# A two-layer encoder trunk: another order of work where the up projections pass into the down projections

## The chip, the cores and the metric

The kernel runs on one core of one Trainium2 chip. A core has TensorE (PE, matrix products), VectorE (DVE), ScalarE (ACT), GpSimd (POOL) and SyncE (SP, whose queue starts most transfers), each with an instruction stream of its own that runs in order; they meet at semaphores. The metric is device time in microseconds (us) of one execution. Before the change three runs gave a median of 2614.29 us (2614.18 to 2615.53).

## The reference, cut to what matters

Each of two layers is a token mixer (attention in the first, a gated delta rule in the second) followed by a dense MLP. The change is at one place inside the MLP, which runs once per layer:

```python
def squared_relu_mlp(h, w_up, w_down):
    return jnp.square(jax.nn.relu(h @ w_up)) @ w_down

x = x + squared_relu_mlp(rmsnorm(x, mlp_norm[i]), mlp_w_up[i], mlp_w_down[i])
```

x is 1024 tokens by 1024, w_up 1024 by 4096, w_down 4096 by 1024, all float32.

## The kernel before

**Products.** Every float32 matrix is split into a high part (rounded by ACT, method `high`, L1017) and a low part (the rest, a subtraction on DVE, method `low`, L1014, or on POOL, L1012). A product of two such matrices is three matmuls: high by high, high by low, low by high. Big products are done in 2 by 2 blocks with seven block products in place of eight, so sums and differences of blocks are needed on both sides: of the weights (`s1` to `s4`, made on POOL by `padd`, L1023, and `psub`, L1020, then split), and of the activations (`t1` to `t4`).

**Up.** `up` works through 16 groups (n = 0 to 15) of 256 of the 4096 hidden features. A group ends with four blocks of squared activations `g`. Three of them go to DRAM as they are (`gr`, issued by ACT); `combine` makes the four sums of them: POOL subtracts (L1020), ACT takes the high part (L1017), DVE the low part (L1093), and SP stores both to DRAM (`gt`, L1094), 512 KB each. The sums of group n are made beside the products of group n+1. Those of the last group, n = 15, have no next group: `block` hands them to `down` as the generator `late`.

**Down.** `down` has 32 units: 8 blocks b of hidden features by 4 pairs u of output panels. A unit has seven block products of 6 matmuls, called slots here: Y 11, Z s1, Y s2, X 12, Y s3, Z s4, Y 22. After each slot, `step` (L1377) lets every side job go one step: `late`, then `work` (loads and splits of the activations of block b+1, method `rows`), then `more` (the weights of the unit after this one, `down_weights`); only then does DVE add the slot's result from PSUM to x (L1419). So whatever a step gives to DVE stands ahead of that addition in DVE's stream. Y collects several products in one PSUM tile, and a slot on Y can start only when DVE has read the tile for the slot before on Y. In slot Z s1 of each unit the low part of the next unit's first weights (`wlo`) is given to DVE ahead of the additions of Z s1 and Y s2. Unit weights arrive as a 512 KB tile `wraw` by SP (L1227); there are two such buffers.

**The passage.** The rows of block b = 0 and the weights of unit 0 are made during the last up group, by the generator `tail` in `block`, one of whose steps is taken at seven places of `up` (method `end`) and one right after it. Its last step asks for the first four x tiles (L2505, 512 KB each); `down` then asks for the weights of unit 1. Each x tile takes the buffer of a sum of group 14, so its load must wait until that sum is stored. The order of SP's queue is set when the program is built; the order on the other engines is that of the code. SP's stream is in order too: an entry that waits for another engine holds all loads and stores behind it.

Of the kernel before, what the change touches and what calls it, by code (L numbers as in the profile page):

```python
# [8 lines left out]
F32 = mybir.dt.float32  # L9
F32R = mybir.dt.float32r  # L10
I32 = mybir.dt.int32
AF = mybir.ActivationFunctionType
ALU = mybir.AluOpType
# [4 lines left out]
P = 128  # L18
D = 1024
S = 1024  # L20
KT = D // P
HB = 512
# [186 lines left out]
class Trunk:  # L209
# [871 lines left out]
    def combine(self, n, g, mp, gt):  # L1081

        nc = self.nc
        t = {z: mp.tile([P, S], F32, name=self.nm("c"), tag=f"x{4 * (n % 2) + k}") for k, z in enumerate(SUMS)}

        def sub(z, x, y):
            self.psub(t[z][:, HB:], x, y)

        def high(z):
            self.high(t[z][:, :HB].bitcast(F32R), t[z][:, HB:])  # L1090

        def low(z):
            nc.vector.tensor_tensor(t[z][:, HB:].bitcast(F32R), t[z][:, HB:], t[z][:, :HB], ALU.subtract)  # L1093
            nc.sync.dma_start(gt[n, SUMS.index(z)], t[z])  # L1094

        sub("t1", g[0, 1], g[0, 0])
        sub("t3", g[1, 1], g[0, 1])
        yield
        sub("t2", g[1, 1], t["t1"][:, HB:])
        sub("t4", g[1, 0], t["t2"][:, HB:])  # L1100
        high("t1")
        yield
        high("t3")
        low("t1")
        yield
        high("t2")
        low("t3")
        yield
        high("t4")
        low("t2")  # L1110
        yield
        low("t4")
        yield
# [107 lines left out]
            A, rest = nxt, more  # L1221
        return sums

    def down_weights(self, i, b, u, ap, A, keep=False):

        raw = self.wp.tile([P, 4, 2, P], F32, name=self.nm("wraw"), tag="wraw")
        self.wq.dma_start(raw, self.a["w_down"][i, b, u])  # L1227
        yield
        hi, lo = (self.wp.tile([P, 4, 2, P], F32R, name=self.nm("w" + z), tag="w" + z) for z in ("hi", "lo"))

        def kept(tag, n=2):
            return [x[:, : n * 2 * P].rearrange("p (n k m) -> p n k m", n=n, k=2) for x in self.part(self.hp, tag)]

        h42, l42 = kept(f"{2 * u}0") if keep else (hi[:, 2:4], lo[:, 2:4])
        A["11"], A["12"] = ((hi[:, n], lo[:, n]) for n in range(2))
        A["s4"], A["22"] = ((h42[:, n], l42[:, n]) for n in range(2))

        self.high(hi[:, 0:2], raw[:, 0:2])
        if keep and u:
            s31, s2 = (x.bitcast(F32) for x in kept(f"{u}1"))  # L1240
            s2 = s2[:, 0]
        else:
            s31 = ap.tile([P, 2, 2, P], F32, name=self.nm("s"), tag="a0")
            s2 = ap.tile([P, 2, P], F32, name=self.nm("s"), tag="a1")
        self.padd(s31[:, 1], raw[:, 2], raw[:, 3])
        self.psub(s2, s31[:, 1], raw[:, 0])
        yield

        self.low(lo[:, 0:2], raw[:, 0:2], hi[:, 0:2])
        yield  # L1250

        yield

        if keep and u:
            A["s2"] = tuple(x[:, 0] for x in kept(f"{(0, 4, 5, 0)[u]}1"))
        else:
            A["s2"] = tuple(ap.tile([P, 2, P], F32R, name=self.nm("a"), tag=f"a{4 + n}") for n in range(2))
        self.high(A["s2"][0], s2)
        self.psub(s31[:, 0], raw[:, 0], raw[:, 2])
        self.psub(raw[:, 2], raw[:, 1], s2)  # L1260
        yield

        self.low(A["s2"][1], s2, A["s2"][0])
        yield

        if keep and u:
            h31, l31 = kept(f"{2 * u + 1}0")
        else:
            h31, l31 = (ap.tile([P, 2, 2, P], F32R, name=self.nm("a"), tag=f"a{2 + n}") for n in range(2))
        A["s3"], A["s1"] = ((h31[:, n], l31[:, n]) for n in range(2))  # L1270
        self.high(h31, s31)
        yield

        self.low(l31, s31, h31, b == 7)
        self.high(h42, raw[:, 2:4])
        yield

        self.low(l42, raw[:, 2:4], h42, b == 7)
        yield
# [82 lines left out]
    def down(self, i, hx, mq, xs, late, gr, gt, ops, first, after, ahead, norm):  # L1362

        nc = self.nc
        units = [(b, u) for b in range(8) for u in range(4)]

        def add(x, y):
            nc.vector.tensor_tensor(x, y, x, ALU.add)

        A, rest = first  # L1370
        nxt = {}
        more = self.down_weights(i, *units[1], hx, nxt)
        next(more)
        work, part = None, None
        ready, doing, at = [], [], [0]

        def step():  # L1377

            at[0] += 1
            early = not part and (G["m_order"] >> (at[0] - 1) % 14) & 1  # L1380
            if early:
                next(more, None)
            next(late, None)
            next(work, None)
            if part:
                for d in doing:
                    next(d)
                doing.clear()
                if ready:
                    x, k, h = ready.pop(0)  # L1390
                    d = part(x, k, h)
                    next(d)
                    doing.append(d)
            if not early:
                next(more, None)
            if n >= 30:
                next(ahead, None)

        for n, (b, u) in enumerate(units):
            if u == 0:  # L1400
                work = iter(())
                if b < 7:
                    work = self.rows(hx, gr, gt, b + 1, ops[(b + 1) % 2])
                else:
                    part = after()
                B = ops[b % 2]
            if norm and b == 7:
                after_next, more = more, iter(())
                next(rest)
                self.down_end(i, hx, mq, xs, B, {0: A, 1: nxt}, {1: after_next}, part, norm)  # L1410
                break
            x11, x12, x21, x22 = (xs[2 * u + m][:, h * HB : (h + 1) * HB] for m in range(2) for h in range(2))
            X = self.bank()
            Y, Z = (mq.tile([P, HB], F32, name=self.nm(z), tag=z) for z in "yz")

            def slot(ps, l, r, first, last, x, k=None, h=None):
                self.block_product(ps, A[l], B[r], first, last)
                step()
                nc.vector.tensor_tensor(x, ps, x, ALU.add)  # L1419
                if part and k is not None:  # L1420
                    ready.append((x, 2 * u + k, h))

            next(rest, None)
            slot(Y, "11", "11", True, False, x11)
            if n < len(units) - 1:
                slot(Z, "s1", "t1", True, False, x22)
                slot(Y, "s2", "t2", False, False, x12)
                slot(X, "12", "21", True, True, x11, 0, 0)
                slot(Y, "s3", "t3", False, False, x22, 1, 1)
                slot(Z, "s4", "22", False, True, x12, 0, 1)  # L1430
                slot(Y, "22", "t4", False, True, x21, 1, 0)
            else:
                slot(X, "12", "21", True, True, x11, 0, 0)
                slot(Y, "s2", "t2", False, False, x12)
                slot(Z, "s1", "t1", True, False, x22)
                slot(Y, "s3", "t3", False, False, x22, 1, 1)
                slot(Z, "s4", "22", False, True, x12, 0, 1)
                slot(Y, "22", "t4", False, True, x21, 1, 0)
            A, rest = nxt, more
            nxt, more = {}, iter(())  # L1440
            if n + 2 < len(units):
                more = self.down_weights(i, *units[n + 2], hx, nxt, bool(norm) and n + 2 >= 28)
                next(more)
        while ready or doing:
            step()
        for _ in ahead:
            pass
# [69 lines left out]
    def block(self, i, rhs, x, w, which, after, done=None, ahead=iter(()), norm=None):  # L1517
# [5 lines left out]
        with tc.tile_pool(name=f"xa{i}", bufs=1) as xa, tc.tile_pool(name=f"xb{i}", bufs=1) as xb, \  # L1523
# [12 lines left out]
            def tail():  # L1536
                rows = self.first_rows(xp, ex, gr, gt, B[0])
                got["A"] = {}
                got["rest"] = weights = self.down_weights(i, 0, 0, hx, got["A"])
                for steps in (1, 1, 2, 1, 2, 1):  # L1540
                    next(rows, None)
                    for _ in range(steps):
                        next(weights)
                    yield
                next(rows, None)
                got["xs"] = self.load_x(xp, xd, range(4))
                yield

            def late():
# [5 lines left out]
            with tc.manual_schedule(engines=ENG):  # L1555
                self.out_proj(w, rhs, xs, tile_done, finish, rest)
                sums = self.up(i, ops, hx, xp, yz, gr, gt, finish, A, rest, end)
                next(end)
                self.down(i, hx, yz, got["xs"], chain(sums, late()), gr, gt, B, (got["A"], got["rest"]),
                          after, ahead, norm)  # L1560
                if done:
                    done(got["xs"])
# [996 lines left out]
```

## Time and profile before

| | |
|---|---|
| runs, median of 3 | 2614.29 us |
| profiled execution, its own time | 2614.47 us |
| its span | 2612.4 us |
| PE busy | 2476.4 us, 95% |
| DVE / ACT / POOL busy | 1922.9 (74%) / 1211.8 (46%) / 1320.8 us (51%) |
| chain that ended last, by engine | PE 76%, DVE 12%, DMA 4%, issue 3%, POOL 2%, ACT 2% |
| passage of the first layer | near 880 to 930 us |
| passage of the second layer | near 2260 to 2310 us |

The last up group of the first layer ends near 889 us and the first unit of `down` begins there; the same work comes again in the second layer near 2268 us. In a row of a timeline the bracket at the end gives how long the engine sat idle before that work and which work ended the wait. The column PEclk is the clock granted to TensorE, 1.00 for 2.4 GHz and 0.50 for 1.2 GHz.

### The profile page before, as it was taken

Reading aid. Unit: us, or ns where it says so; the run is one execution under the profiler, and the core shown is the slowest. Engines: PE = TensorE matmul, PEld = TensorE weight load, DVE = VectorE, ACT = ScalarE, POOL = GpSimd, SP = SyncE. Lnnn points to the kernel's source line nnn. Section 1 sums busy time; section 2 is a strip of 40 time slices with the busy share of each in tenths; the row PEclk is TensorE's granted clock in tenths of the full one; section 3 lists DMA queues with packets and bytes.
Section 4 is the critical chain, followed back from the end, with each engine's and each line's share of the span. In section 5 each row is a group of like instructions: output and inputs, shape, how many; then the busy total and the mean of one; then the engine's idle time right before and its main releaser. Section 6 shows DMA issues by size and latency. Waiting matters only on the chain.

```text
span 2612.4 us, 36716 instructions
## 1 busy us (share of the span) xinstructions
PE 2476.4 (95%) x12638; PEld 2067.2 (79%) x12638; DVE 1922.9 (74%) x3287; ACT 1211.8 (46%) x2269; POOL 1320.8 (51%) x1100
## 2 busy tenths in 40 slices
PE   8999999989999899998888999999889999899997
PEld 6888888877888678886666788888777888688885
DVE  6665656677878778878578976676677787778887
ACT  5666667534555433234673343343335455533333
POOL 2444456236676656565464333332225666565656
PEclk9999999999999999999998999999999999999998
DMA  4222224315555876643443121222324555876652
GB/s 159 69 67 77 60 84 155 116 73 181 213 208 207 309 261 203 230 145 108 117 139 111 55 73 59 68 81 105 105 89 157 206 214 207 301 265 221 215 164 81
DMA packets 189050, 389.28 MB, mean 149 GB/s; under 512 B 54512, under 2 KB 61104, under 8 KB 188864
## 3 DMA queue, kind: packets, MB, share of 16 engines
q1 hardware_dynamic: 172592, 353.36, 39.9%
q10 hardware_dynamic: 16272, 33.58, 3.3%
q8 instruction: 99, 1.62, 0.3%
q14 instruction: 87, 0.71, 0.1%
HBM read 251.96 MB, written 126.52 MB: 145 GB/s over the span
## 4 chain that ended last, share of the span: by engine, by line
PE 76%; DVE 12%; DMA 4%; issue 3%; POOL 2%; ACT 2%; SPq 1%; DVEq 0%; ACTq 0%; POOLq 0%
PE y L1008 23%; PE acc L164 17%; PE z L1008 11%; PE acc L1008 6%; PE tp L164 3%; PE s L164 3%; PE po L164 2%; PE pt L164 2%; PE sp L164 2%; PE acc L279 2%; PE acc L280 2%; PE acc L278 2%; DVE ft L164 2%; DVE wlo L1014 1%; DMA xs<-gt 1%
## 5 line engine op out<-in xcount | busy, mean ns | idle before, releaser
L164 PE MATMUL acc<-xs,whi 128*128 128x512 f32 x1808 | 629.1, 411 | 9.7 <-DVE xp L164 7.2
L164 PEld LDWEIGHTS acc<-xs,whi 128*128 128x128 f32 x1808 | 331.6, 190 | 59.0 <-DVE xp L164 7.9
L164 PE MATMUL acc<-xs,wlo 128*128 128x512 f32 x896 | 367.0, 410 | 2.8 <-POOL wlo L164 2.8
L1008 PE MATMUL y<-xs,whi 128*128 128x512 f32 x1008 | 316.9, 396 | 9.2 <-DVE ssum L1127 9.2
L164 POOL TENSOR_TENSOR wlo<-wraw,whi 128x512 fp32r<-128x512 f32 x126 | 167.7, 1331 | 246.3 <-ACT whi L164 197.9
L1023 POOL TENSOR_TENSOR s<-wraw 128x256 f32<-128x256 f32 (+1 forms) x93 | 91.4, 983 | 357.9 <-DVE a L1014 180.4
L1014 DVE TENSOR_TENSOR wlo<-wraw,whi 128x512 fp32r<-128x512 f32 (+1 forms) x184 | 212.5, 1155 | 44.6 <-ACT whi L1017 44.6
L1008 PEld LDWEIGHTS y<-xs,whi 128*128 128x128 f32 x1008 | 192.9, 192 | 51.0 <-DVE ssum L1127 10.4
L1008 PE MATMUL y<-xs,a 128*128 128x512 f32 x732 | 192.0, 398 | 22.9 <-DVE x L1419 22.9
L1008 PE MATMUL y<-xs,wlo 128*128 128x512 f32 x504 | 200.0, 397 | 12.9 <-DVE wlo L1014 12.9
L1017 ACT ACTIVATE whi<-wraw 128x512 fp32r<-128x512 f32 (+2 forms) x191 | 146.4, 767 | 129.9 <-PE y L1008 83.7
L1419 DVE TENSOR_TENSOR x<-y,x 128x512 f32<-128x512 f32 x240 | 165.4, 689 | 41.1 <-PE y L1008 27.8
L1017 ACT ACTIVATE a<-s 128x256 fp32r<-128x256 f32 x122 | 64.0, 525 | 282.6 <-PE y L1008 167.0
L164 PEld LDWEIGHTS acc<-xs,wlo 128*128 128x128 f32 x896 | 170.7, 190 | 28.3 <-POOL wlo L164 4.4
L1008 PEld LDWEIGHTS y<-xs,a 128*128 128x128 f32 x732 | 139.0, 191 | 56.7 <-DVE x L1419 25.7
L1093 DVE TENSOR_TENSOR c<-c 128x512 fp32r<-128x512 f32 x128 | 151.9, 1206 | 36.2 <-POOL c L1020 35.7
L1008 PE MATMUL acc<-xs,whi 128*128 128x512 f32 x528 | 164.2, 392 | 0.0
L1008 PE MATMUL y<-xs,ahi 128*128 128x512 f32 x512 | 158.6, 391 | 2.0 <-ACT nt L1148 2.0
L164 POOL TENSOR_SCALAR pr<-pr,rs 128x640 f32<-128x640 f32 (+4 forms) x128 | 88.1, 691 | 129.2 <-DVE rs L164 98.1
L1008 PE MATMUL z<-xs,whi 128*128 128x512 f32 x480 | 150.3, 395 | 0.0
L164 POOL TENSOR_TENSOR cy<-cy,cz 128x512 f32<-128x512 f32 x48 | 68.9, 1436 | 144.4 <-DVE cz L164 131.0
L1020 POOL TENSOR_TENSOR c<-g,ssum 128x512 f32<-128x512 f32 x32 | 41.4, 1295 | 184.4 <-ACT g L1130 179.4
(320 smaller groups left out, 6341.0 us busy)
## 6 DMA issues: line engine op xcount, KB each, us to landing
gt<-c SPq DMA_DIRECT2D x128, 512.0 KB, 2.8
xs<-gt SPq DMA_DIRECT2D x256, 256.0 KB, 4.4
wraw<-in_w_up_dram SPq DMA_DIRECT2D x64, 512.0 KB, 3.4
wraw<-in_w_down_dram SPq DMA_DIRECT2D x64, 512.0 KB, 4.3
r<-gr SPq DMA_DIRECT2D x96, 256.0 KB, 3.1
gr<-ssum ACTq DMA_DIRECT2D x64, 256.0 KB, 2.3
wraw<-in_w_in_dram SPq DMA_DIRECT2D x32, 512.0 KB, 3.4
wraw<-in_w_qkv_dram SPq DMA_DIRECT2D x30, 512.0 KB, 3.3
```

Source lines behind the costliest of these rows:

```text
L164: return call(*args, **more)
L278: nc.tensor.matmul(ps, hi[:, k], xh, start=(k == 0), stop=False)
L279: nc.tensor.matmul(ps, hi[:, k], xl, start=False, stop=False)
L280: nc.tensor.matmul(ps, lo[:, k], xh, start=False, stop=(k == KT - 1))
L1008: nc.tensor.matmul(ps, w[:, k], x, start=bool(first and f), stop=bool(last and e), skip_group_check=True)
L1014: self.nc.vector.tensor_tensor(lo, src, hi.bitcast(F32), ALU.subtract)
L1017: self.nc.scalar.activation(hi, src, AF.Copy)
L1020: self.nc.gpsimd.tensor_tensor(out, x, y, ALU.subtract)
L1023: self.nc.gpsimd.tensor_tensor(out, x, y, ALU.add)
L1093: nc.vector.tensor_tensor(t[z][:, HB:].bitcast(F32R), t[z][:, HB:], t[z][:, :HB], ALU.subtract)
L1419: nc.vector.tensor_tensor(x, ps, x, ALU.add)
```

## The change

It has five parts, all at the passage, in both layers:

- `down_weights` gets a branch for unit 0 (`start=True`): the same sums, high and low parts, but the four POOL operations in a row, then s2 and the s1/s3 pair split first, the plain blocks last. `tail` takes one step of it per step of its own.
- `tail` asks for x tiles 0 and 1 after its fifth step, then for the weights of unit 1, then for x tiles 2 and 3. `down` gets unit 1's weights handed in instead of asking for them.
- `late` (the sums of group 15, then x tiles 4 to 7) starts at `down`'s third step instead of its first.
- In `combine`, for group 15 alone, the low parts of `t1` and `t3` move from DVE to POOL.
- Nothing is left out or added in the arithmetic; PE's order stays as it was.

```diff
@@ combine
         def low(z):
-            nc.vector.tensor_tensor(t[z][:, HB:].bitcast(F32R), t[z][:, HB:], t[z][:, :HB], ALU.subtract)
+            eng = nc.gpsimd if z in ("t1", "t3") and n == 4 * KT // 2 - 1 else nc.vector
+            eng.tensor_tensor(t[z][:, HB:].bitcast(F32R), t[z][:, HB:], t[z][:, :HB], ALU.subtract)
             nc.sync.dma_start(gt[n, SUMS.index(z)], t[z])
@@ down_weights
+        if start:
...
+            self.padd(s31[:, 1], raw[:, 2], raw[:, 3])
+            self.psub(s2, s31[:, 1], raw[:, 0])
+            self.psub(s31[:, 0], raw[:, 0], raw[:, 2])
+            self.psub(raw[:, 2], raw[:, 1], s2)
+            yield
...
+            self.high(A["s2"][0], s2)
+            self.low(A["s2"][1], s2, A["s2"][0])
+            self.high(h31, s31)
+            yield
+            self.low(l31, s31, h31)
+            self.high(hi[:, 0:2], raw[:, 0:2])
+            yield
+            self.low(lo[:, 0:2], raw[:, 0:2], hi[:, 0:2])
+            self.high(h42, raw[:, 2:4])
+            yield
+            self.low(l42, raw[:, 2:4], h42)
+            yield
+            return
@@ down
-        A, rest = first
-        nxt = {}
-        more = self.down_weights(i, *units[1], hx, nxt)
-        next(more)
+        A, rest, nxt, more = first
...
-            next(late, None)
+            if at[0] > 2:
+                next(late, None)
@@ block
-                got["rest"] = weights = self.down_weights(i, 0, 0, hx, got["A"])
-                for steps in (1, 1, 2, 1, 2, 1):
+                weights = self.down_weights(i, 0, 0, hx, got["A"], start=True)
+                for n in range(6):
                     next(rows, None)
-                    for _ in range(steps):
-                        next(weights)
+                    next(weights)
+                    if n == 4:
+                        got["xs"] = self.load_x(xp, xd, range(2))
                     yield
-                next(rows, None)
-                got["xs"] = self.load_x(xp, xd, range(4))
+                got["next"] = {}
+                got["more"] = self.down_weights(i, 0, 1, hx, got["next"])
+                next(got["more"])
+                got["xs"] += self.load_x(xp, xd, range(2, 4))
                 yield
```

What this does to the order is shown at three places of the first layer; the second layer has the same rows under other numbers.

POOL, from the first sums of group 15 (c_9334 is t1, c_9336 t3, c_9335 t2, c_9337 t4; wraw_9322 the weights of unit 1, s_... their sums; xs and r the rows of block b = 1), before:

```order
L1020 TENSOR_TENSOR c_9334<-g_6866,ssum_6864 128x512
L1020 TENSOR_TENSOR c_9336<-ssum_6864,g_6866 128x512
L1023 TENSOR_TENSOR s_9349<-wraw_9322 128x256
L1020 TENSOR_TENSOR s_9350<-s_9349,wraw_9322 128x256
L1020 TENSOR_TENSOR c_9335<-ssum_6864,c_9334 128x512
L1020 TENSOR_TENSOR c_9337<-g_6865,c_9335 128x512
L1012 TENSOR_TENSOR xs_9363<-r_9340,xs_9363 128x512
L1020 TENSOR_TENSOR s_9349<-wraw_9322 128x256
L1020 TENSOR_TENSOR wraw_9322<-wraw_9322,s_9350 128x256
```

and of the change (t1 is c_9364, t3 c_9366, t2 c_9365, t4 c_9367, unit 1's weights wraw_9319):

```order
L1023 TENSOR_TENSOR s_9343<-wraw_9319 128x256
L1020 TENSOR_TENSOR s_9344<-s_9343,wraw_9319 128x256
L1020 TENSOR_TENSOR c_9364<-g_6866,ssum_6864 128x512
L1020 TENSOR_TENSOR c_9366<-ssum_6864,g_6866 128x512
L1012 TENSOR_TENSOR xs_9354<-r_9334,xs_9354 128x512
L1020 TENSOR_TENSOR s_9343<-wraw_9319 128x256
L1020 TENSOR_TENSOR wraw_9319<-wraw_9319,s_9344 128x256
L1020 TENSOR_TENSOR c_9365<-ssum_6864,c_9364 128x512
L1020 TENSOR_TENSOR c_9367<-g_6865,c_9365 128x512
L1094 TENSOR_TENSOR c_9364<-c_9364 128x512
L1012 TENSOR_TENSOR xs_9386<-r_9336,xs_9386 128x512
L1094 TENSOR_TENSOR c_9366<-c_9366 128x512
```

All four sums now stand behind the first sums of unit 1's weights, and the two low parts behind the four sums.

SP, from the second x tile to the first store of group 15 (one x tile stands ahead of the first row in each), before:

```order
L2505 DMA x_9316<-xd_6091 128x1024
L2505 DMA x_9318<-xd_6091 128x1024
L2505 DMA x_9320<-xd_6091 128x1024
L1227 DMA wraw_9322<-in_w_down_dram 128x1024
L1347 DMA r_9340<-gr_6089 128x512
L1347 DMA r_9342<-gr_6089 128x512
L1347 DMA r_9344<-gr_6089 128x512
L1227 DMA wraw_9439<-in_w_down_dram 128x1024
L1337 DMA xs_9465<-gt_6090 128x512
L1094 DMA gt_6090<-c_9334 128x1024
```

and of the change:

```order
L2533 DMA x_9298<-xd_6091 128x1024
L1229 DMA wraw_9319<-in_w_down_dram 128x1024
L2533 DMA x_9321<-xd_6091 128x1024
L2533 DMA x_9323<-xd_6091 128x1024
L1373 DMA r_9334<-gr_6089 128x512
L1373 DMA r_9336<-gr_6089 128x512
L1373 DMA r_9338<-gr_6089 128x512
L1229 DMA wraw_9429<-in_w_down_dram 128x1024
L1363 DMA xs_9465<-gt_6090 128x512
L1364 DMA xs_9465<-gt_6090 128x512
L1363 DMA xs_9486<-gt_6090 128x512
L1095 DMA gt_6090<-c_9364 128x1024
```

Unit 1's weights pass two x tiles, and two half loads of block 1's rows pass ahead of the stores. Behind the first store the queue has in both kernels the other three stores, x tiles 4 to 7, the rest of those half loads (five before, three now) and the weights of unit 3. What stands ahead of the first x tile is the same in both but for one pair that changes places.

DVE, the first additions of `down` (x_9314 and x_9316 are x tiles 0 and 1; y, z and acc the PSUM tiles Y, Z and X), before:

```order
L1419 TENSOR_TENSOR x_9314<-y_9325,x_9314 128x512
L1014 TENSOR_TENSOR wlo_9347<-wraw_9322,whi_9346 128x512
L1419 TENSOR_TENSOR x_9316<-z_9326,x_9316 128x512
L1093 TENSOR_TENSOR c_9334<-c_9334 128x512
L1419 TENSOR_TENSOR x_9314<-y_9325,x_9314 128x512
L1093 TENSOR_TENSOR c_9336<-c_9336 128x512
L1419 TENSOR_TENSOR x_9314<-acc_9324,x_9314 128x512
```

and of the change:

```order
L1443 TENSOR_TENSOR x_9296<-y_9326,x_9296 128x512
L1014 TENSOR_TENSOR wlo_9341<-wraw_9319,whi_9340 128x512
L1443 TENSOR_TENSOR x_9298<-z_9327,x_9298 128x512
L1443 TENSOR_TENSOR x_9296<-y_9326,x_9296 128x512
L1443 TENSOR_TENSOR x_9296<-acc_9325,x_9296 128x512
L1014 TENSOR_TENSOR a_9379<-s_9344,a_9378 128x256
L1443 TENSOR_TENSOR x_9298<-y_9326,x_9298 128x512
L1443 TENSOR_TENSOR x_9296<-z_9327,x_9296 128x512
L1094 TENSOR_TENSOR c_9365<-c_9365 128x512
L1014 TENSOR_TENSOR a_9413<-s_9343,a_9412 128x512
```

The low part of t1 no longer stands ahead of the addition for Y s2; that of unit 1's weights still does. The low part of t2 now stands ahead of the s1/s3 pair of unit 1.

## Rows read from the trace of the kernel before

**Rows 1.** Waits of PE, 860 to 960 us: total us, times, longest.

```profile
PE y L1008 <- DVE x L1419: 9.4, 4, 5.0
```

**Rows 2.** Timeline of PE, first layer: start, duration, work, [idle before <- releaser].

```profile
895.18 2.31 PE L1008 MATMUL y<-xs,a 128*128 128x512 f32 x6 [2.58 <-DVE x L1419]
...
904.73 2.93 PE L1008 MATMUL y<-xs,a 128*128 128x512 f32 x6 [4.95 <-DVE x L1419]
...
912.58 1.52 PE L1008 MATMUL z<-xs,a 128*128 128x512 f32 x6
...
925.96 0.39 PE L1008 MATMUL acc<-xs,wlo 128*128 128x512 f32 x1
927.90 1.66 PE L1008 MATMUL y<-xs,a 128*128 128x512 f32 x6 [1.55 <-DVE x L1419]
```

**Rows 3.** Timeline of DVE, first layer.

```profile
894.43 0.69 DVE L1419 TENSOR_TENSOR x<-y,x 128x512 f32<-128x512 f32 x1 [2.50 <-DMA x<-xd]
900.84 0.69 DVE L1014 TENSOR_TENSOR wlo<-wraw,whi 128x512 fp32r<-128x512 f32 x1 [5.72 <-ACT whi L1017]
...
903.38 0.69 DVE L1093 TENSOR_TENSOR c<-c 128x512 fp32r<-128x512 f32 x1 [1.25 <-POOL c L1020]
903.99 0.68 DVE L1419 TENSOR_TENSOR x<-y,x 128x512 f32<-128x512 f32 x1
```

**Rows 4.** Timeline of ACT, both layers.

```profile
900.18 0.63 ACT L1017 ACTIVATE whi<-wraw 128x512 fp32r<-128x512 f32 x1 [8.18 <-DMA wraw<-in_w_down_dram]
...
925.29 0.63 ACT L1017 ACTIVATE whi<-wraw 128x512 fp32r<-128x512 f32 x1 [6.09 <-DMA wraw<-in_w_down_dram]
...
2303.00 0.63 ACT L1017 ACTIVATE whi<-wraw 128x512 fp32r<-128x512 f32 x1 [4.77 <-DMA wraw<-in_w_down_dram]
```

**Rows 5.** Timeline of POOL, first layer.

```profile
892.08 1.27 POOL L1020 TENSOR_TENSOR c<-g,ssum 128x512 f32<-128x512 f32 x1 [11.13 <-ACT g L1130]
893.31 1.26 POOL L1020 TENSOR_TENSOR c<-ssum,g 128x512 f32<-128x512 f32 x1
900.23 0.72 POOL L1023 TENSOR_TENSOR s<-wraw 128x256 f32<-128x256 f32 x1 [5.66 <-DMA wraw<-in_w_down_dram]
901.04 1.09 POOL L1020 TENSOR_TENSOR s<-s,wraw 128x256 f32<-128x256 f32 x1
902.08 1.27 POOL L1020 TENSOR_TENSOR c<-ssum,c 128x512 f32<-128x512 f32 x1
903.43 1.78 POOL L1020 TENSOR_TENSOR c<-g,c 128x512 f32<-128x512 f32 x1
905.17 1.73 POOL L1012 TENSOR_TENSOR xs<-r,xs 128x512 fp32r<-128x512 f32 x1
906.86 1.18 POOL L1020 TENSOR_TENSOR s<-wraw 128x256 f32<-128x256 f32 x1
908.12 0.80 POOL L1020 TENSOR_TENSOR wraw<-wraw,s 128x256 f32<-128x256 f32 x1
```

**Rows 6.** Timeline of SP's queue, both layers: start, time over all issues, transfer.

```profile
904.10 5.77 SPq L1094 DMA_DIRECT2D gt<-c  x4
...
2283.22 5.76 SPq L1094 DMA_DIRECT2D gt<-c  x4
```

**Rows 7.** DMA issues on the page: KB each, median us from issue to landing.

```profile
gt<-c SPq DMA_DIRECT2D x128, 512.0 KB, 2.8
```

**Rows 8.** Windows, first layer: length, busy by engine, PEclk, DMA share, GB/s.

```profile
905.00:909.60 4.60, 4.60 (x12) 3.54 (x13) 4.52 (x6) 2.41 (x4) 4.52 (x5) 0.50 0.81 333
910.00:920.00 10.00, 10.00 (x45) 8.24 (x45) 7.54 (x12) 2.21 (x4) 6.17 (x6) 1.00 0.95 325
920.00:930.00 10.00, 8.45 (x37) 6.67 (x37) 6.08 (x11) 3.21 (x6) 4.52 (x5) 1.00 1.05 407
```

**Rows 9.** Timeline of PE, second layer.

```profile
2283.84 2.93 PE L1008 MATMUL y<-xs,a 128*128 128x512 f32 x6 [4.30 <-DVE x L1419]
...
2305.61 1.66 PE L1008 MATMUL y<-xs,a 128*128 128x512 f32 x6 [0.24 <-DVE x L1419]
```

More of the change, by code (lines that the diff above doesn't have):

```diff
@@ L1222, in up, with down_weights @@
         return sums
-    def down_weights(self, i, b, u, ap, A, keep=False):
+    def down_weights(self, i, b, u, ap, A, keep=False, start=False):
         raw = self.wp.tile([P, 4, 2, P], F32, name=self.nm("wraw"), tag="wraw")
@@ L1236, in down_weights @@
         A["s4"], A["22"] = ((h42[:, n], l42[:, n]) for n in range(2))
+        if start:
+            s31 = ap.tile([P, 2, 2, P], F32, name=self.nm("s"), tag="a0")
+            s2 = ap.tile([P, 2, P], F32, name=self.nm("s"), tag="a1")
+            self.padd(s31[:, 1], raw[:, 2], raw[:, 3])
[3 more added lines that the diff above has]
+            yield
+            A["s2"] = tuple(ap.tile([P, 2, P], F32R, name=self.nm("a"), tag=f"a{4 + n}") for n in range(2))
+            h31, l31 = (ap.tile([P, 2, 2, P], F32R, name=self.nm("a"), tag=f"a{2 + n}") for n in range(2))
+            A["s3"], A["s1"] = ((h31[:, n], l31[:, n]) for n in range(2))
+            self.high(A["s2"][0], s2)
[11 more added lines that the diff above has]
+            return
         self.high(hi[:, 0:2], raw[:, 0:2])
@@ L1558, in block @@
                 next(end)
-                self.down(i, hx, yz, got["xs"], chain(sums, late()), gr, gt, B, (got["A"], got["rest"]),
+                self.down(i, hx, yz, got["xs"], chain(sums, late()), gr, gt, B,
+                          (got["A"], iter(()), got["next"], got["more"]),
                           after, ahead, norm)
```

## The prediction

> **What bounds the kernel now.** I read the waits of PE first, then PE's timeline at the passage, and from each idle stretch went to the engine that ended it, and on to what that engine had waited for. PE is what the kernel runs on; at the first layer's passage it waits 9.4 us for DVE's additions to x, in four waits [rows 1]. Three of them matter [rows 2]: 2.58 us ahead of Y s2 of unit 0, 4.95 us ahead of its Y s3, 1.55 us ahead of Y s3 of unit 2. In the second layer the last two are 4.30 and 0.24 us [rows 9].
>
> Each ends on something else. The first ends on the landing of the first x tile (DVE at 894.43) [rows 3]. The second has two causes in a row: DVE holds the low part of unit 1's weights, which land only at 900.18 (DVE idles 5.72 us), and then the low part of t1, for which it waits on POOL until 903.38; the addition that PE needs comes at 903.99 [rows 3, 4, 5]. The third is the same kind of wait for the weights of unit 3, which land at 925.29 [rows 4]. From there to PE's Y s3 it is 2.61 us, in the first layer (927.90) as in the second (2303.00 to 2305.61) [rows 2, 4, 9]. So there is a second bound behind the first: however early PE gets through units 0 to 2, it can't start Y s3 of unit 2 before unit 3's weights have landed and 2.61 us have passed.
>
> Those weights stand in SP's queue behind the four stores of group 15, and these stores set when SP goes on. In the first layer the first store is issued at 904.10, as DVE ends the low part of t1 (903.38 + 0.69), and the four take 5.77 us [rows 3, 6].
>
> **The change part by part.** The sum is made against the profiled execution, 2614.47 us, 0.18 us over the median of the runs.
>
> *Unit 0's weights in another order.* Same operations, ahead of the first x tile's landing. That tile's place in SP's queue is practically unchanged, so the wait of 2.58 us ends when it did and hides a shift of a few tenths either way: 0. "x asked for sooner" is so in the code alone; in the queue only unit 1's weights move.
>
> *Unit 1's weights sooner.* They pass two x tiles, 1.05 MB. At the 407 GB/s of a stretch with a full queue [rows 8] that is 2.6 us, so they land at 897.6. With the sums of group 15 out of DVE's way as well, Y s3 of unit 0 can start after one high part, one low part and two additions (0.63 + 0.69 + 0.68 + 0.68) [rows 3, 4]: 900.3 in place of 904.73, 4.4 us sooner. The clock adds to that: after the wait of 4.95 us PE worked at 0.50 until 909.6 [rows 2, 8], which cost half of 4.87 us, 2.4 us.
>
> *The sums later, and two low parts on POOL.* POOL did the sums t1 and t3 at 892.08, while it had nothing else to do; now they stand behind unit 1's weights. From 897.6 POOL has in its stream, with the durations of rows 5: 0.72 + 1.09 for unit 1, 1.27 + 1.26 for t1 and t3, 1.73 for a row's low part, 1.18 + 0.80 for unit 1, 1.27 + 1.78 for t2 and t4. That is 11.1 us, to 908.7. Only then comes the low part of t1. The trace has none of these on POOL; the nearest rows of its form are 1.27 us (a sum with DVE idle) and 1.73 to 1.78 us (beside DVE), and I take 1.5. The first store is issued at 910.2, 6.1 us later than before. The low part of t3 needs another 1.73 + 1.5, so the second store goes at 913.4; t2 and t4 are then ready on DVE (their high and low parts take 0.63 and 0.69) and follow at once.
>
> What is queued behind these stores is x tiles 4 to 7, three half loads, and the weights of unit 3. From 913.4 SP's queue has to move 3 stores (1.57 MB), 4 x tiles (2.10), 3 halves (0.79) and the weights (0.52): 4.98 MB. The two windows of 10 us in which these moved before show 325 and 407 GB/s [rows 8]; at their mean, 366, it takes 13.6 us. A store alone lands 2.8 us after issue [rows 7], of which 1.4 is its 0.52 MB at that rate, so 1.4 is start-up. Unit 3's weights land at 913.4 + 1.4 + 13.6 = 928.4, 3.1 us later than 925.29. The ends are 1.7 (407 GB/s) and 4.8 us (325 GB/s). In the second layer the same chain gives a first store at 2283.22 + 6.1 [rows 6], the second 3.2 later, the landing at 2307.5, 4.5 us later than 2303.00 (ends 3.1 and 6.2).
>
> *What becomes late next.* One wait comes earlier: the s1/s3 pair of unit 1 on ACT and DVE now stands behind the high and low parts of t2, whose sum ends on POOL at 906.9. With two further high parts and the low part (about 2.7 us) Z s1 of unit 1 starts near 909.7, not 912.58 [rows 2], so 4.4 us of gain are down to 2.9 there. At Y s3 of unit 2 the rest is gone: it starts 2.61 us after the weights, at 931.0 and 2310.1, 3.1 and 4.5 us later than before.
>
> *The clock.* Ahead of it PE idles at least as long as the block is late plus the old wait: 1.55 + 3.1 and 0.24 + 4.5, that is 4.7 us in each layer. The nearest row, 4.95 us of idling, was followed by work at 0.50 that cost 2.4 us; idling of 1.55 us by none, as the six matmuls right after it took 1.66 us [rows 2]. I take 2.1 per layer, ends 0 and 2.4.
>
> *The sum.* 3.1 + 4.5 + 2 × 2.1 = 11.8 us on 2614.47, so 2626.3 us. The low ends give 1.7 + 3.1 + 0 = 4.8 us (2619.3), the high ends 4.8 + 6.2 + 4.8 = 15.8 us (2630.3). The rest of `down` runs on PE with hardly a wait, so nothing behind gives it back.
>
> **The rivals.**
>
> *Faster: the gain is kept.* If unit 3's weights came sooner by as much as PE does, each layer would keep 4.4 + 2.4 us: the first 6.8, the second, with an idle stretch shorter by 0.65, 6.1; 2614.5 − 12.9 = 2601.6 us. For it: SP's queue ran dry behind the first store's wait, and the store itself isn't urgent. Against it: the landing would have to come over 5 us before 925.29, and that asks for a first store before 904.10, while POOL has 11 us of work ahead of it from 897.6.
>
> *No change: the queue catches up.* The four stores were issued over 5.77 us before and three of them go at once now; if the queue then stays full at over 407 GB/s, the weights land within a microsecond of the old time, and the old bound holds: at best the waits of 1.55 and 0.24 us go, 2612.7 us, and with a landing 1 to 2 us late in each layer it is some 2617 us. I put this case at 2615.
>
> *Slower by more: POOL stretched.* POOL's operations take 1.27 us alone and up to 1.78 beside DVE [rows 5]. If each of the eight of 128 by 512 up to t3's low part meets an operation of DVE in full, each takes 1.27 + 0.69 = 1.96 us, 15.7 in place of the 12.0 in my chain. That is 3.6 us more per layer, 2633.5 us. The decisive point is whether DVE has work at 898 to 913, and it idles part of it. The Trainium skill, page "SBUF — State Buffer", section "Who interferes with whom", says that GpSimd and a two-input DVE instruction take turns on a shared pair of ports, as an exclusive lock; by it this rival is the rule, while the rows, with 1.73 to 1.78, stay under the full sum, so the trace agrees in part.
>
> **How the numbers follow.** A difference under 0.2%, 5.2 us, counts as none for this kernel (2609.1 to 2619.5). The forecast gets 0.66 (2619.3 to 2630.3, likeliest 2626.3), the stretched POOL 0.08, no change 0.13, the kept gain 0.13. So slower 0.74, same 0.13, faster 0.13. The range of 2610 to 2633 leaves out the kept gain and half of the stretched case, under 2 in 10.
>
> **What would show it.** Right: unit 1's weights reach ACT near 897.6 and Y s3 of unit 0 starts near 900.3 with hardly a wait; the first store of group 15 is issued near 910 and 2289, after POOL; ACT's high part of unit 3's weights near 928.4 and 2307.5; an idle stretch of PE of 4 us or more ahead of Y s3 of unit 2, by the addition behind that low part, and a window at 0.50 behind it. Wrong: a first store before 906, weights of unit 3 before 926, or no clock loss at unit 2. If the stores are late and the weights of unit 3 are not, the step from stores to weights has failed; if both are late and the time hasn't grown, the claim that nothing behind gives it back has.

## The result and the profile after

The changed kernel takes 2621.92 us (median of 8 runs, 2620.07 to 2624.58); the kernel before, run beside it, 2614.34 us (2611.37 to 2617.09). The ratio is 1.0032 with a 95% interval of 1.0023 to 1.0041: 7.6 us slower, more than the 0.2% that can be told here. The forecast was 2626.3 us, slower. The profiled execution took 2620.07 us, 5.6 us over that of before.

PE's timeline at both passages (start, duration, work, [idle before <- what ended it]):

```profile
883.37 0.73 PE L1008 MATMUL y<-xs,whi 128*128 128x512 f32 x2 [3.17 <-DVE ssum L1128]
...
898.53 1.67 PE L1008 MATMUL y<-xs,a 128*128 128x512 f32 x6 [1.93 <-DVE x L1443]
...
906.29 0.73 PE L1008 MATMUL z<-xs,a 128*128 128x512 f32 x2 [1.96 <-ACT a L1017]
909.40 2.07 PE L1008 MATMUL z<-xs,a 128*128 128x512 f32 x4 [2.37 <-DVE a L1014]
913.36 2.93 PE L1008 MATMUL y<-xs,a 128*128 128x512 f32 x6 [1.89 <-DVE x L1443]
...
928.85 1.65 PE L1008 MATMUL y<-xs,a 128*128 128x512 f32 x6 [0.39 <-DVE x L1443]
...
2265.10 0.74 PE L1008 MATMUL y<-xs,whi 128*128 128x512 f32 x2 [3.30 <-DVE ssum L1128]
...
2311.34 1.66 PE L1008 MATMUL y<-xs,a 128*128 128x512 f32 x6 [0.51 <-DVE x L1443]
```

Against [rows 2, 9]: the wait of 4.95 us ahead of Y s3 of unit 0 is down to 1.93, and that slot starts at 898.53 in place of 904.73. Three new waits stand at unit 1 (906.29 to 913.36, 6.2 us in all; 2.00, 2.37 and 1.89 us in the second layer), and the six matmuls behind the last of them take 2.93 us where others take 1.65. At Y s3 of unit 2 (928.85, 2311.34) PE waits 0.39 and 0.51 us.

The first row of each layer, the last sum of the up projections, gives a point to count from. The kernel before has it here:

```profile
884.14 0.73 PE L1008 MATMUL y<-xs,whi 128*128 128x512 f32 x2 [1.78 <-DVE ssum L1127]
...
2264.08 0.73 PE L1008 MATMUL y<-xs,whi 128*128 128x512 f32 x2 [1.50 <-DVE ssum L1127]
```

From there to Y s3 of unit 2 it was 927.90 − 884.14 = 43.76 and 2305.61 − 2264.08 = 41.53 us; now it is 45.48 and 46.24. So the passages cost 1.7 and 4.7 us, 6.4 in sum. I call this the passage length below. It leaves out that PE gets to that last sum 1.3 us sooner than before and then waits longer for it (1.78 to 3.17 us, 1.50 to 3.30). Counted from a matmul some 9 us ahead of it, where both kernels still run alike (875.48 and 874.60 in the first layer, 2255.71 and 2256.19 in the second), the passages cost 1.8 and 5.2 us, 7.1 in sum, nearer to the 7.6 of the medians. Nothing behind gives it back: the slot on Y at 944.96 starts 0.94 us later now, as Y s3 of unit 2 does (0.95).

Where it comes from, on ACT (the high parts of the weights of units 1 and 3; rows like [rows 4]):

```profile
895.92 0.63 ACT L1017 ACTIVATE whi<-wraw 128x512 fp32r<-128x512 f32 x1 [3.06 <-DMA wraw<-in_w_down_dram]
...
926.23 0.63 ACT L1017 ACTIVATE whi<-wraw 128x512 fp32r<-128x512 f32 x1 [4.92 <-DMA wraw<-in_w_down_dram]
...
2308.73 0.63 ACT L1017 ACTIVATE whi<-wraw 128x512 fp32r<-128x512 f32 x1 [5.07 <-DMA wraw<-in_w_down_dram]
```

on POOL and DVE in the first layer (like [rows 5, 3]):

```profile
904.61 1.27 POOL L1020 TENSOR_TENSOR c<-g,c 128x512 f32<-128x512 f32 x1
905.83 1.29 POOL L1094 TENSOR_TENSOR c<-c 128x512 fp32r<-128x512 f32 x1
907.08 1.71 POOL L1012 TENSOR_TENSOR xs<-r,xs 128x512 fp32r<-128x512 f32 x1
908.76 1.72 POOL L1094 TENSOR_TENSOR c<-c 128x512 fp32r<-128x512 f32 x1
```

```profile
905.92 1.76 DVE L1094 TENSOR_TENSOR c<-c 128x512 fp32r<-128x512 f32 x1 [3.60 <-POOL c L1020]
907.60 1.75 DVE L1014 TENSOR_TENSOR a<-s,a 128x512 fp32r<-128x512 f32 x1
909.26 0.68 DVE L1443 TENSOR_TENSOR x<-y,x 128x512 f32<-128x512 f32 x1
```

and in SP's queue (like [rows 6]):

```profile
907.15 5.94 SPq L1095 DMA_DIRECT2D gt<-c  x4
...
918.17 0.51 SPq L1229 DMA_DIRECT2D wraw<-in_w_down_dram  x1
...
2289.46 5.94 SPq L1095 DMA_DIRECT2D gt<-c  x4
```

Unit 1's weights come 4.3 us sooner in the first layer, 1.1 in the second (on ACT at 2278.19 in place of 2279.29). In the first layer POOL then works without a gap to 907.12, where the low part of t1 ends, and the first store leaves at 907.15, 3.05 us later than before (6.24 in the second layer). Unit 3's weights land at 926.23 and 2308.73, and PE starts Y s3 2.62 and 2.61 us behind them. DVE stands idle for 3.60 us: next in its stream is the low part of t2 (905.92), which overwrites t2 and so waits until POOL has read t2 for the sum t4. The part of unit 1's weights that Z s1 needs (907.60) stands behind it.

While SP waits with the store at the head of its queue, the transfers run dry. Windows of the first layer (busy by engine, granted clock, DMA share, GB/s), before and after:

```profile
895.00:905.00 10.00, 4.87 (x13) 3.58 (x14) 3.04 (x6) 3.64 (x7) 4.61 (x4) 0.72 0.75 297
905.00:915.00 10.00, 10.00 (x35) 8.00 (x36) 9.24 (x13) 3.04 (x5) 9.84 (x9) 0.77 0.82 305
```

```profile
895.00:905.00 10.00, 7.40 (x32) 5.36 (x30) 4.44 (x7) 3.57 (x7) 8.79 (x9) 1.00 0.76 301
905.00:915.00 10.00, 4.45 (x10) 2.82 (x11) 8.59 (x8) 2.80 (x6) 9.92 (x8) 0.68 0.51 206
```

In the second pair POOL is full (9.92 of 10 us) while PE works 4.45 us and the DMA engines stand half idle: the missing share, times the length, is 7.3 us of dry time in these 20 us, against 4.3 before.

### The profile page after: what moved, and what is told of

It reads as the page before. It is cut to its first block, busy times and chain, and to the rows that moved or that the text cites. A ratio compares the mean times of both kernels' runs of the same rounds, so it can differ in the third digit from the quotient of the medians.

```text
span 2618.1 us, 36706 instructions
## 1 busy us (share of the span) xinstructions
PE 2480.5 (95%) x12638; PEld 2070.5 (79%) x12638; DVE 1924.6 (74%) x3283; ACT 1211.8 (46%) x2269; POOL 1321.4 (50%) x1104
## 4 chain that ended last, share of the span: by engine, by line
PE 78%; DVE 12%; DMA 3%; issue 3%; POOL 2%; ACT 2%; SPq 0%; DVEq 0%; ACTq 0%; POOLq 0%
PE y L1008 24%; PE acc L164 17%; PE z L1008 11%; PE acc L1008 6%; PE tp L164 4%; PE s L164 3%; PE po L164 2%; PE pt L164 2%; PE sp L164 2%; PE acc L279 2%; PE acc L280 2%; PE acc L278 2%; DVE ft L164 1%; DVE wlo L1014 1%; DMA row<-grows 1%
## 5 line engine op out<-in xcount | busy, mean ns | idle before, releaser
L164 DVE CUSTOM_DVE_ANT_0 pr<-sp,bias 128x640 f32<-128x640 f32 (+4 forms) x128 | 83.9, 655 | 63.9 <-PE sp L164 62.9
```

What stands on the lines that cost most here:

```text
L164: return call(*args, **more)
```

## The experiments

Two theories to begin with. *Queue*: the time is set by unit 3's weights, behind the stores in SP's queue. *Passage*: PE loses it itself, at Z s1 of unit 1. All times are medians, each ratio is to the kernel before, run beside it; an interval reaches some 2 to 4 us to either side.

**e1: unit 3's weights on another queue.**

```diff
-        self.wq.dma_start(raw, self.a["w_down"][i, b, u])
+        (self.nc.scalar if (b, u) == (0, 3) else self.wq).dma_start(raw, self.a["w_down"][i, b, u])
```

> The changed kernel, with the weights of unit 3 of the first half asked for on ACT's queue (behind ACT's high parts of unit 1) in place of SP's, where they stand behind the four stores. Queue theory (the lateness is that of unit 3's weights behind the stores): the high part of unit 3's weights comes on ACT before 920 and 2300 in place of 926.23 and 2308.73, PE does not wait at Y s3 of unit 2, and the time falls by most of what the weights came later, 0.9 + 5.7 us, to about 2615. Passage theory (PE itself came late through Z s1 of unit 1, by its new waits of 1.96, 2.37 and 1.89 us and work at the half clock around them): the weights come sooner all the same, but PE waited for them only 0.39 and 0.51 us, so at most 0.9 us of time goes, 2621.

2625.00 us, 1.0044 (1.0032 to 1.0057). Neither theory's number, because the edit did the opposite of what was meant. ACT's stream is in order too, and the request stands behind a high part that waits for PE:

```profile
919.86 0.63 ACT L1017 ACTIVATE a<-s 128x512 fp32r<-128x512 f32 x1 [3.32 <-PE y L1008]
919.97 0.37 ACTq L1229 DMA_DIRECT2D wraw<-in_w_down_dram  x1
920.39 0.61 ACT L1017 ACTIVATE whi<-wraw 128x512 fp32r<-128x512 f32 x1
927.66 0.63 ACT L1017 ACTIVATE whi<-wraw 128x512 fp32r<-128x512 f32 x1 [6.65 <-DMA wraw<-in_w_down_dram]
```

Asked for at 919.97, not 918.17, the weights land 1.4 us later, PE's wait at Y s3 of unit 2 grows from 0.39 to 2.10 us (0.51 to 1.61 in the second layer), and 3.1 us are lost. Later weights cost time; whether sooner ones give it back was left open.

**e2, e3, e4: undo the late sums, the two low parts on POOL, or both.** e2 and e4 drop the condition, e3 and e4 drop the choice of engine:

```diff
-            if at[0] > 2:
-                next(late, None)
+            next(late, None)
...
-            eng = nc.gpsimd if z in ("t1", "t3") and n == 4 * KT // 2 - 1 else nc.vector
+            eng = nc.vector
```

> The changed kernel without the condition that holds the last sums back for two steps; the low parts of t1 and t3 stay on POOL. Queue theory: t1 and t3 are summed on POOL before unit 1's weights land (near 893, as before the change), their low parts follow by 896, all four stores are issued 3 us or more before 907.15 and 2289.46, unit 3's weights land as much sooner, and the time falls to 2612 to 2617. Passage theory: the two low parts on POOL (1.3 to 1.7 us each) still stand ahead of unit 1's other sums or beside DVE, so the waits of PE at Z s1 of unit 1 stay at 4 us or more, and the time stays within 3 us of 2621.9.

2620.60 us, 1.0027 (1.0016 to 1.0039): hardly better. The Z s1 waits are gone, but the first store leaves at 902.31 and the other three only at 907.80, behind t3's low part on POOL. At Y 22 of unit 0 PE waits 2.78 and 2.75 us for DVE instead, and then in each layer for the weights, with a half clock behind it:

```profile
928.61 2.93 PE L1008 MATMUL y<-xs,a 128*128 128x512 f32 x6 [5.67 <-DVE x L1442]
...
2309.86 2.93 PE L1008 MATMUL y<-xs,a 128*128 128x512 f32 x6 [4.66 <-DVE x L1442]
```

ACT has the weights at 926.00 and 2307.25, 2.61 us ahead of both. So the passage theory alone falls: PE comes to that slot 5.67 and 4.66 us before it may start, and the time stays.

> The changed kernel with the low parts of t1 and t3 on DVE again; the sums stay held back. Queue theory: the first store no longer stands behind 9.9 us on POOL but behind the sum t1 (ends 899.1 on POOL) and DVE, so it is issued near 900.5 in place of 907.15; but the last two, t2 and t4, still end on POOL at 905.9 or a little sooner, so the fourth store leaves near 909, some 4 us sooner than the 913.1 of the changed kernel; unit 3's weights come 2 to 4 us sooner and the time falls to 2615 to 2618. Passage theory: POOL loses 1.29 + 1.72 us, DVE gets 0.7 to 1.2 us twice, the stretch in which the two hold each other up (1.7 us per operation from 905.9 to 912) shrinks, PE's waits at Z s1 fall from 6.2 us to about 4, and the time falls by 2 to 4 us, to about 2619.

2621.52 us, 1.0034 (1.0022 to 1.0046): both theories expected 2 to 7 us of gain and there is none. The first three stores leave from 904.28, the fourth at 912.21; PE waits 5.54 us for DVE at Y 22 of unit 0 and 2.57 us at Y s3 of unit 2, 2.61 us behind the weights (925.30); in the second layer 4.17 and 2.79 us:

```profile
906.33 1.22 PE L1008 MATMUL y<-xs,whi 128*128 128x512 f32 x2 [5.54 <-DVE x L1443]
...
927.91 2.65 PE L1008 MATMUL y<-xs,a 128*128 128x512 f32 x6 [2.57 <-DVE x L1443]
...
2312.38 1.66 PE L1008 MATMUL y<-xs,a 128*128 128x512 f32 x6 [2.79 <-DVE x L1443]
```

> The changed kernel with the sums as before the change (from the first step on, all low parts on DVE): what is left is unit 0's weights made in another order and unit 1's weights and x asked for in another order. Queue theory: the stores are issued no later than before the change (904.10, 2283.22), the weights of unit 3 land as before or a little sooner, Y s3 of unit 0 keeps its 4 us, and the second bound (2.61 us behind unit 3's weights) holds: 2610 to 2614. Passage theory: with no sums beside it Z s1 of unit 1 has no new wait, and the time is the same or less, 2608 to 2614. Both expect that it does not stay at 2621.9; if it does, the order of the weights costs the time and not the sums.

2610.60 us, 0.9986 (0.9977 to 0.9995). With both undone the rest of the change gains 3.6 us. Each of the two alone gives that back and 6 to 7 us more, and the two together cost little more than either. Each alone also makes unit 3's weights late: counted from the last sum they land after 39.76 and 37.44 us in e4, 42.12 and 41.07 in e2, 42.44 and 43.40 in e3, 42.86 and 43.63 in the changed kernel (41.15 and 38.92 before). In e4 PE waits for them as well, if less:

```profile
924.48 2.72 PE L1008 MATMUL y<-xs,a 128*128 128x512 f32 x6 [2.89 <-DVE x L1442]
...
2302.45 1.66 PE L1008 MATMUL y<-xs,a 128*128 128x512 f32 x6 [1.53 <-DVE x L1442]
```

**e5 to e8: unit 3's weights ahead of x tiles 4 to 7.** The same edit in four kernels; it moves four transfers in SP's queue and nothing on another engine.

```diff
             def late():
+                for _ in range(20):
+                    yield
                 for k in range(4, KT):
...
                 next(more)
+            if n == 1:
+                for _ in late:
+                    pass
```

> The changed kernel with unit 3's weights ahead of x tiles 4 to 7 in SP's queue; the order on every other engine stays. They are then asked for some 3 us sooner and land 3 to 5 us sooner, near 922 and 2304 in place of 926.23 and 2308.73. Weights theory (only this landing holds PE up): the time falls by as much as the landing, 3 to 5 us in each layer, to 2612 to 2616. Two-bounds theory (PE, held up by its waits of 1.96, 2.37 and 1.89 us at unit 1, gets to Y s3 of unit 2 only 0.39 and 0.51 us before the weights): at most these 0.9 us go, 2621. Next-in-line theory (x tiles 4 to 7 are as late as the weights were): PE waits for x at the start of unit 2 instead, 2622 or more.

2620.11 us, 1.0022 (1.0014 to 1.0031), 1.8 us less than the changed kernel, which is not clear of the noise. The weights are on ACT at 922.46 and PE no longer waits for them, yet the waits at unit 1 stay (2.39 and 2.29 us, six matmuls at 2.93), and in the first layer ACT then waits 5.82 us for the next rows in the same late queue. That is the two-bounds theory's number, within what can be told.

> The kernel of e2 (sums from the first step, low parts of t1 and t3 on POOL; 2620.6 us) with unit 3's weights ahead of x tiles 4 to 7. There PE has no wait at unit 1 and idles 5.67 and 4.66 us ahead of Y s3 of unit 2. Weights theory and two-bounds theory both: weights 3 to 5 us sooner give these 3 to 5 us in each layer, and a part of the work at the half clock behind them, so 2610 to 2614. Next-in-line theory: the waits move to the x tiles, 2619 to 2622. Against e5 it tells the first two apart: a gain here and none there shows two bounds in the changed kernel.

2616.93 us, 1.0011 (1.0002 to 1.0019): 3.7 us less than e2, a gain where e5 had half of it, though under the 6 to 10 expected. PE's wait of 5.67 us is gone, that of 4.66 is down to 2.23, which ends on the next in line, an x tile (DVE, second layer):

```profile
2305.38 0.69 DVE L1442 TENSOR_TENSOR x<-y,x 128x512 f32<-128x512 f32 x1 [2.87 <-DMA x<-xd]
```

> The kernel of e4 (weights' order and requests alone; 2610.6 us) with unit 3's weights ahead of x tiles 4 to 7. PE waits there 2.89 and 1.53 us at Y s3 of unit 2, and its six matmuls behind the first take 2.72 us in place of 1.65. Weights and two-bounds theory: the waits go and the first one's half clock with them, 4.4 us and 1 to 2 us, so 2604 to 2606, the fastest of all. Next-in-line theory: x tiles 4 and 5, needed at the start of unit 2, come 1 to 2 us later and PE waits for them, 2609 to 2612.

2608.06 us, 0.9973 (0.9964 to 0.9982), 6.5 us under the kernel before; of e4's waits at Y s3 of unit 2 (2.89 and 1.53 us) none is left. 2 to 4 us less gain than expected: ahead of Y s3 of unit 0 PE waits 3.73 and 3.79 us for DVE, which makes low parts of the sums there.

> The kernel before with nothing changed but unit 3's weights ahead of x tiles 4 to 7. Weights and two-bounds theory: of PE's waits only 1.55 and 0.24 us end on these weights, so 2612 to 2613. Next-in-line theory: no gain, 2614 to 2616. It also says how much of e7's gain is due to this edit alone.

2611.16 us, 0.9990 (0.9981 to 0.9999): 3.4 us of gain, 1.6 more than the two waits account for, which the interval covers.

**e9: all four sums ahead of unit 1's weights.**

```diff
             next(late, None)
+            if at[0] == 1:
+                next(late, None)
```

> The kernel of e7 (2608.1 us) with the second step of the last sums taken together with the first, so that POOL has all four sums behind it before unit 1's weights land, and the low parts, all on DVE, stand ahead of those weights' low part. Idle-queue theory (what costs or gains time is how long the 16 DMA engines stand idle while SP waits for the first store: from 895 to 915 us their share is 0.75 and 0.82 before the change, 0.76 and 0.51 after it, 0.82 and 0.99 in e4, 0.78 and 1.00 in e7): the first store leaves near 896 in place of 899.82, the fourth near 901 in place of 905.2, the share is 0.95 or more in both windows, and the time falls by another 2 to 4 us, to 2604 to 2606. Rival (once unit 3's weights are ahead of x, PE's own waits at unit 0 are the bound): four low parts of 0.7 us on DVE and four high parts of 0.6 us on ACT now stand ahead of Y s2 or s3 of unit 0 and PE waits there as long as it does in e7 (3.7 us per layer) or longer, so 2607 to 2611.

2607.38 us, 0.9968 (0.9955 to 0.9980), the same as e7. The stores do leave sooner (897.78) and the queue is full, with 1.1 us dry in place of e7's 2.2:

```profile
895.00:905.00 10.00, 5.26 (x17) 3.86 (x16) 7.93 (x10) 5.11 (x10) 9.76 (x9) 0.84 0.89 360
905.00:915.00 10.00, 10.00 (x44) 8.00 (x43) 7.62 (x11) 2.56 (x5) 5.74 (x6) 0.99 1.00 347
```

PE waits 4.74 us at Y s3 of unit 0 instead (e7: 3.73; in the second layer 3.59 and 3.79). The rival is right: with unit 3's weights out of the way, dry time is no longer the bound.

**e10: the kernel before with the late sums alone** (its `next(late, None)` under `if at[0] > 2`).

> The kernel before with the condition of the change alone: the last sums begin two steps later, all else is as before. Idle-queue theory: POOL's sums stand behind unit 1's weights, which land at 900.2 here, so the first store goes 6 us or more after 904.10, the DMA engines idle that much longer, unit 3's weights land 4 to 6 us later and with PE's wait there the time is 2621 to 2626, slower than the changed kernel, which has the weights of unit 1 sooner. Rival (the sums cost nothing where they are, the loss comes from unit 0's and unit 1's new order together with them): 2613 to 2617.

2623.11 us, 1.0037 (1.0023 to 1.0051), as expected in size, not in its way. The stores leave at 909.48 to 917.40, but in the first layer PE doesn't wait for unit 3's weights at all; it had lost 5.55 us at 911.51, at Y 22 of unit 0, for an addition of DVE that stands behind the late low part of t2. In the second layer it waits 3.07 us there and 0.33 us for the weights.

**e11: e7 with unit 0's weights in the old order** (`start=True` left out, with the old steps of `tail`).

> The kernel of e7 (2608.1 us) with unit 0's weights made in the old order; unit 1's weights and x are still asked for in the new order, and unit 3's ahead of x tiles 4 to 7. If the other order of unit 0's weights is worth nothing, as predicted: the same within 1.5 us, 2606.5 to 2609.5. If it is what lets PE start unit 0 sooner: 2610 or more. If it costs (before the last sum of the up projections PE waits 3.2 us in the changed kernel where it waited 1.8 us, for an addition of DVE that the low parts of unit 0 now stand ahead of): 2604 to 2606.

2607.27 us, 0.9974 (0.9965 to 0.9984): the same as e7. PE's wait for the last sum is 1.50 us in place of 2.75 in the first layer, and the wait ahead of Y s2 of unit 0, 2.80 us, takes it back.

**e12: the kernel before with the two low parts on POOL alone** (the choice of engine from the change).

> The kernel before with one thing changed: the low parts of t1 and t3 of the last sums are made on POOL in place of DVE. On POOL t3's low part stands behind t2, t4, t1's low part, a row's low part and the last two of unit 1's sums. With the durations of e2, where these stand in the same order (1.29 for t1's, 1.71 for the row, 0.91 + 1.13 for unit 1, 1.78 for t3's), the second store goes some 6 us behind the first, near 911 in place of 905.5, and the other two with it; four stores end 3 us later than 909.87. If the queue behind the stores carries that on: unit 3's weights come 3 us later in each layer, PE waits for them 4.5 and 3.2 us at Y s3 of unit 2 and then works a while at the half clock, 2620 to 2625. If DVE, rid of two low parts of 0.7 to 1.2 us, gives PE its additions of unit 0 sooner and so makes up for it: 2612 to 2616.

2628.66 us, 1.0055 (1.0041 to 1.0069), 14.2 us slower, beyond what was expected. SP's queue:

```profile
906.12 6.31 SPq L1095 DMA_DIRECT2D gt<-c  x3
912.53 0.67 SPq L2506 DMA_DIRECT2D x<-xd  x1
913.29 1.09 SPq L1095 DMA_DIRECT2D gt<-c  x1
915.87 3.62 SPq L2506 DMA_DIRECT2D x<-xd  x3
...
923.44 0.38 SPq L1228 DMA_DIRECT2D wraw<-in_w_down_dram  x1
```

POOL makes t3's low part only at 909.82 (1.79 us), the store of it and all behind it wait for that, and unit 3's weights are asked for 7.4 us later than at 916.03. ACT has them at 929.52 and 2315.29, and PE:

```profile
932.13 2.93 PE L1008 MATMUL y<-xs,a 128*128 128x512 f32 x6 [6.77 <-DVE x L1420]
...
2317.90 2.93 PE L1008 MATMUL y<-xs,a 128*128 128x512 f32 x6 [7.79 <-DVE x L1420]
```

The passage lengths are 48.60 and 48.68 us, 4.8 and 7.2 more than before; the six matmuls at the half clock add 1.3 us twice, 14.6 in sum, against 14.2 measured. Here the queue accounts for all of it.

## Why the prediction was right, and where it failed

*Unit 0's reorder, 0.* Right in sum: e11 and e7 differ by 0.8 us, within their intervals. The shift it hides is not a few tenths, though: in the first layer the wait ahead of the last sum is 1.25 us longer in e7 than in e11.

*Unit 1's weights sooner.* Right in kind; in the first layer 4.3 us sooner (2.6 forecast), Y s3 of unit 0 at 898.53 (900.3), in the second only 1.1 us. With the sums left as they were it gains 3.6 us (e4). In e7 it is 6.5, of which e8 gets 3.4 from that edit alone. So a gain as in "kept gain", the first rival, was there, a good quarter of the 12.9 us put on it, and the other half of the change is what took it.

*From POOL to the first store.* The order was right and the length a little short of the forecast: 9.9 us from the landing to the low part of t1, not 11.1. DVE was idle from 902.32 to 905.92, and the sum t4 took 1.27 us in place of 1.78; the last two of unit 1's sums took 0.73 each in place of 1.18 and 0.80, and the row's low part 1.48 in place of 1.73. The store left at 907.15 and 2289.46 (910.2 and 2289.3 forecast). "POOL stretched" therefore didn't happen.

*From the stores to unit 3's weights, and from there to Y s3 of unit 2.* Right. The landings are 926.23 and 2308.73 (928.4 and 2307.5), the passages cost 1.7 and 4.7 us (3.1 and 4.5), 6.4 in place of 7.6. That PE cannot start Y s3 earlier than 2.61 us behind this landing held wherever PE waited there: 15 passages of before, after, e1 to e4, e10 and e12, all 2.60 to 2.62 us. e2 and e12 show it as cause: there PE comes to that slot 4.66 to 7.79 us before it may start, and the kernels are 6.4 and 14.2 us slower than before.

*The clock, 4.2 us.* This step failed, and with it the sum of 11.8 us. It was put as "Ahead of it PE idles at least as long as the block is late plus the old wait". PE idled 0.39 and 0.51 us there, not 4.7, and nothing behind ran at the half clock, which the prediction itself had named as a sign against it. It had Z s1 of unit 1 near 909.7, and 909.40 is where most of it started; but it booked this as a smaller gain and didn't go on from there. DVE and ACT, in order, stood waiting for POOL's sums; PE idled 6.2 us in three pieces and worked at the half clock from 909.40 to 918.60 (granted clock 0.50; four matmuls in 2.07, six in 2.93 us), and so came to Y s3 of unit 2 only 0.4 us before it might start. So the clock did cost time, but on PE's way to the weights, where it adds nothing to the wait for them. There are two bounds of nearly equal lateness: PE's own, from the late sums, and the weights', which the late sums or the low parts on POOL make late, each alone (e3, e2). e5 takes the weights away and gains 1.8 us; e2 takes the waits at unit 1 away and gains 1.3, neither clear of the noise; both, in e6, gain 5.0. That 2621.92 lies in the range is partly luck: the low end had the clock at 0, the passages alone make up what was measured, and nothing in the prediction made PE as late as the weights. Where PE does arrive early, in e2 and e12, the clock term is there, 1.3 us in the six matmuls alone.

Two points stay open. Low parts on POOL still cost 8.9 us between e7 and e6. PE's waits over 0.3 us at the two passages add up to 21.0 us in e6 and 14.4 in e7; e6 has 3.42 and 2.77 us at Y 22 of unit 0, 1.59 at Y 22 of unit 2 and the 2.23 for the x tile, none of which e7 has, but no run takes them away one by one. And in e10 PE is late by itself, with the weights at most 0.33 us behind; no run says what it would gain if DVE's order alone were mended.

## What to carry to other kernels

When work is put off, ask two things of it: what its product holds up in an in-order queue, and which engine will have to stand waiting for it with urgent work behind. Each can be the bound by itself, so undoing one shows little; try them together. And where a queue is full after a stall, put the one transfer that PE waits for ahead of those with slack: here that, with the sums early and their low parts on DVE, gives the fastest kernels (2607 to 2608 us, 6.5 to 7 us under the kernel before).

## What the runs showed of the hardware that was not expected

DVE and POOL slow each other more than the rows shown of before. DVE's 128x512 low parts took 1.76 and 1.75 us beside POOL at 905.92 and 907.60, where alone they take 0.69, and POOL's took 1.71 and 1.72 in place of 1.27 to 1.29. The rest of the trace of before has it too: the low parts of `combine` go up to 1.79 us there, and POOL's sum t2 takes 1.26 us at the shortest, 2.27 at the median of 32. The Trainium skill, page "SBUF — State Buffer", section "Who interferes with whom", calls the ports that the two share an exclusive lock. The trace agrees in kind: DVE loses 1.07 us to an operation of POOL that takes 1.29 alone. It also shows the other side: POOL's operations at 907.08 and 908.76 start while one of DVE's still runs, and lose 0.4 us each.

Idling of one length does not always cost the clock: in e3 a wait of 2.57 us was followed by six matmuls in 2.65 us, one of 2.79 us by six in 1.66.
